# Early table entries and gathers placed later, the last logits placed before the early products, and a weight prefetch placed before later table entries

## The chip, the core and the metric

The kernel runs on one core of a Trainium2 chip. The metric is the device time of one execution in microseconds, the median of the runs shown. The core has five engines, each with its own queue of instructions that it works through in order: PE (matrix products), DVE (vector operations), ACT (activations and copies), POOL (here mostly DMAs with computed addresses) and SP, which issues the ordinary DMAs. All DMAs run on 16 DMA engines.

## What is computed

One layer of a diffusion backbone over 1024 latent tokens and 256 context tokens of width 1024: two token mixers (a state-space scan and windowed attention), an output projection with a gated residual, and then a mixture of 32 experts. Only the last two matter here:

```python
x = x + g1 * (concatenate([ssd_x, attn_x], axis=-1) @ w_out)
h2 = rms_norm(x, norm2) * (1 + sc2) + sh2
# each token: the best of 4 groups, then the best 2 of its 8 experts
g_prob = softmax(h @ w_group + b_group);  g_w, g_idx = top_k(g_prob, 1)
e_w, e_idx = top_k(softmax(e_logits[g_idx]), 2)
expert = g_idx * 8 + e_idx
# per expert, over its tokens, weighted and summed back into the tokens
y = (silu(xb @ w_gate[e]) * (xb @ w_up[e])) @ w_down[e]
return rms_norm(x + g2 * moe_x, norm_final)
```

All is float32; `w_gate`, `w_up` and `w_down` hold 32 experts with 6 MB each.

## The kernel before

The tokens stand in 8 blocks of 128. `out_all` (L966) is the output projection and the routing. For each block `b`, `out_a` prepares the operands of block `b + 1`; `out_b` (L900) makes the 48 products of the projection on PE, adds the residual on DVE (L912, L913), stores the rows into `acc` (L914), takes the root mean square on ACT (L918, L919), scales the rows on DVE (L920, L922), adds a shift (L923, on POOL, for the last block on DVE) and stores them into `h2d` (L924). `out_c` (L945), called one block behind, transposes the rows on PE (L949), copies them to SBUF (L951, L953), makes the router's logits (L956) and adds their bias on DVE (L957).

`route_to` routes the blocks in three groups that end before blocks 4, 6 and 8. `route` finds each token's two experts and its place among the expert's tokens, and POOL scatters one entry (token, weight) for each into a table in DRAM, `tab`, with one indirect DMA (L1093) for each block and choice: 8, 4 and 4 of them. `counts` counts the tokens of each expert; `place_ranks` sorts the experts by this count on DVE (L1118 to L1128) into a list `ovf`. For all places but the first two, the expert is known only from this list: SP reads it into a register (`expert_at`), both for a weight load and for a load of table entries.

The first two places are always experts 0 and 1 (`FIXED = 2`). They are worked on early, for the tokens of blocks 0 to 3 alone: `early_tables` loads their entries of `tab` with four DMAs on SP (L1237), `early_gather` computes row numbers on DVE (L1241) and gathers the rows of `h2d` on POOL (L1273), `early_x` transposes them, `early_gu` makes their gate and up products on PE (L1304, 64 instructions in the profile for each expert). Experts 0 and 1 get a second place for the tokens of blocks 4 to 7 (numbers 33 and 34), so the places are worked on in the order 0, 1, 33, 34, 2, 3, 4 and so on. A place has 64 slots ("half", two DMAs for its entries) or 128 (one DMA).

Weights come in chunks of 1 MB, six for each expert (two of gate, two of up, two of down), loaded on SP (L1256) into 7 buffers `wr` and 6 buffers `wl`. `prefetch(k)` issues loads in the order of use up to the k-th chunk, as long as by the program's own count a buffer is free. `wl` takes the space of the projection's weights and exists only after the last block. 7 chunks are asked for during the blocks and 12 right behind them, which are all chunks of experts 0 and 1. The chunks of full places are then split into two parts on ACT (L184) and DVE (L185); half places use them as they are.

`moe` (L1537) follows: it loads the entries of 33 and 34 (`tables_to(2 * FIXED)`), the gate `g2` and `g2h`, then `early_rest` finishes the early products (silu L1314, multiply L1315, transposes L1323, down products L1332, weighting L1337, add to `acc` by an indirect DMA L1341) and calls `place_ranks` between the multiply and the transposes. Then come the gathers of 33 and 34, table entries of further places, and the steps of the expert stage, of which each product step calls `prefetch` for all chunks again and gives buffers free.

The order of the instructions on a queue is drawn up when the program is built. A scheduler takes, for each engine, what is ready by its own estimate of the times, and of several the one that stands first in the code. So the order in the code is a priority and not the order itself. What touches the same tile or DRAM tensor waits for what stands before it in the code: a scatter into `tab` waits for an earlier load from it.

Of the kernel before, what the change touches and what calls it, by code (L numbers as in the profile page):

```python
# [21 lines left out]
NBX = NT // P  # L22
# [20 lines left out]
NX, TABLE_AHEAD = 3, 3  # L43
# [17 lines left out]
FIXED, MID, REST = 2, 13, 14  # L61
# [4 lines left out]
EARLY, NVX = 4, NE + FIXED  # L66
# [63 lines left out]
class Kern:  # L130
# [834 lines left out]
    def out_all(self):  # L965
        part, h2 = self.out_a(0), None  # L966
        self.out_mod()
        for b in range(NBX):
            nxt = self.out_a(b + 1) if b + 1 < NBX else None
            if b + 2 < NBX:  # L970
                self.out_load(b + 2)
            if b == EARLY + 2:
                self.early_gather()
            n2 = self.out_b(b, part)
            self.prefetch(min(NR, (3 * b + 4) // 2))
            if h2 is not None:
                self.out_c(b - 1, h2)
                self.route_to(b)
            if b == EARLY + 1:
                self.early_tables()  # L980
            part, h2 = nxt, n2
        self.oa.close()
        self.wop.close()
        self.wl = self.pool("wl", "right")
        self.prefetch(FIXED * NCH)
        self.early_x()
        self.early_gu(0, 0, 2)
        self.out_c(NBX - 1, h2)
        self.early_gu(0, 2, 4)
        self.early_gu(1, 0, 1)  # L990
        self.route_to(NBX)
        self.counts()
        self.early_gu(1, 1, 4)


    def first_max(self, dst_m, dst_i, src, m, n):
# [541 lines left out]
    def moe(self):  # L1538
        blocks = [b for _, bl in self.items for b in bl]
        at = lambda q: self.items[q][1]  # L1540
        X, A, T, Y, Z, G = {}, {}, {}, {}, {}, {}
        done = rows = tabs = FIXED
        nb = len(blocks)
        add = lambda b: self.half_add(Z.pop(b), b) if self.half(b) else self.y_add(Z.pop(b), self.lst[:, b, :])

        def x_ahead(q):

            for b in at(q):
                k = blocks.index(b)
                X[b] = self.half_x(k) if self.half(b) else self.x_t(k)  # L1550
                rows_to(k + NX + 1)
                gather_to(k + NX + 1)
                rows_to(k + NX + 2)
                tables_to(k + NX + 1 + TABLE_AHEAD)

        def gather_to(n):
            nonlocal done
            for i in range(done, min(n, nb)):
                self.gather(i, self.lst[:, blocks[i], :], blocks[i])
                done = i + 1  # L1560

        def rows_to(n):
            nonlocal rows
            for i in range(rows, min(n, nb)):
                self.half_rows(blocks[i])
                rows = i + 1

        def tables_to(n):
            nonlocal tabs
            for i in range(tabs, min(n, nb)):  # L1570
                self.lst_load(blocks[i])
                tabs = i + 1

        tables_to(2 * FIXED)
        self.g2 = self.mod_load(self.mp, 3, "g2")
        self.g2h = self.mp([512], "g2h")
        for n in range(2):
            self.nc.sync.dma_start(out=self.g2h[n * H:n * H + H], in_=self.modd[3][None, n * 512:n * 512 + 512].to_broadcast([H, 512]))
        self.early_rest()
        rows_to(2 * FIXED)  # L1580
        gather_to(2 * FIXED)
        tables_to(FIXED + NX + 1 + TABLE_AHEAD)
        x_ahead(FIXED)
        for t in self.steps:
            k, q = t[0], t[1] if len(t) > 1 else None
            p = self.items[q][0] if q is not None else None
            if k == "gu":
                if q == FIXED + 1 and t[2] == 0:
                    self.overflow()
                if t[2] == 0:  # L1590
                    for b in at(q):
                        G[b] = self.bank2(name="pgu")
                wg, wu = self.parts_for(p, (2 * t[2], 2 * t[2] + 1), (0, 0, 2, NW)[t[2]])
                for b in at(q):
                    if self.half(b):
                        self.half_gu(t[2], X[b], *((wg, wu) if self.half(p) else (wg[2], wu[2])), G[b])
                    else:
                        self.gu(t[2], X[b], wg, wu, G[b])
            elif k == "act":
                for b in at(q):  # L1600
                    A[b] = (self.half_act if self.half(b) else self.act)(G.pop(b))
            elif k == "x":
                x_ahead(q)
            elif k == "hT":
                for b in at(q):
                    T[b] = (self.half_h if self.half(b) else self.h_t)(A.pop(b))
                    Y[b] = self.bank2(name="py")
            elif k == "down":
                w, = self.parts_for(p, (8 + t[2],), 0)
                for b in at(q):  # L1610
                    if self.half(b):
                        self.half_down(T[b], w if self.half(p) else w[2], Y[b], t[2])
                    else:
                        self.down(T[b], w, Y[b], t[2])
            elif k == "y":
                for b in at(q):
                    Z[b] = self.half_y(Y.pop(b), b) if self.half(b) else self.y_out(Y.pop(b), self.lst[:, b, :])
                    if p != REST - 1:
                        add(b)
            elif k == "rest":  # L1620
                self.moe_rest()
                self.rested = True
                for b in list(Z):
                    add(b)
            elif k == "final":
                self.final()
            elif k == "last":
                self.final_rows(Y.pop(p))
# [249 lines left out]
```

## Time and profile before

| | |
|---|---|
| time, median of 3 runs | 1314.62 us (1313.06 to 1315.48) |
| the profiled execution, its own time | 1314.99 us |
| its span, first to last instruction | 1313.2 us |
| PE busy | 1175.0 us (89%) |
| DVE busy | 801.9 us (61%) |
| ACT busy | 577.9 us (44%) |
| POOL busy | 338.8 us (26%) |
| DMA, mean over the span | 255 GB/s, 335.08 MB |
| mean granted clock of TensorE | 0.957 of full speed |

How to read it: the profile is of one execution, times are from the span's start. "PE busy" counts a product from its start to a modelled end. In a timeline a row is one instruction or a run of like ones: start, duration, engine, line of the kernel, operation, "output<-inputs" by the program's names, count, and in brackets how long the engine had stood idle before it and what ended that. For SP the rows are DMA issues; the duration is that of the issue, not of the transfer. In a table of windows each row is a stretch of time with the busy time of each engine, the granted clock of TensorE (1.00 is 2.4 GHz, 0.50 is 1.2 GHz), the share of the DMA engines' time and the rate.

### The profile page before, as it was taken

How to read it: one execution, taken by the hardware profiler on the slowest of the kernel's cores; microseconds unless marked ns; L12 is line 12 of the kernel's file. 1: busy time of each engine (PE TensorE's matmuls, PEld its weight loads, DVE VectorE, ACT ScalarE, POOL GpSimd, SP SyncE). 2: the span in 40 equal slices, each digit the busy share in tenths (PEclk: the TensorE clock that was granted, in tenths of full speed). 3: DMA queues.
4: the chain of work that ended last, by engine and by line, in shares of the span. 5: the costliest groups of instructions: out<-in, count | busy, mean ns of one | idle time of the engine just before them, and what ended most of it. 6: DMA issues, size and time to landing. Idle time of an engine off the chain costs nothing. (4 is left out here: it accounts for less than half of the span.)

```text
span 1313.2 us, 19111 instructions
## 1 busy us (share of the span) xinstructions
PE 1175.0 (89%) x6806; PEld 845.4 (64%) x6806; DVE 801.9 (61%) x1392; ACT 577.9 (44%) x1046; POOL 338.8 (26%) x295
## 2 busy tenths in 40 slices
PE   5799999888798999899997989999999999989881
PEld 2678778878786666588764556555556665556550
DVE  1688885678957877565566525454546545566543
ACT  5643333355547766433340423343334443454423
POOL 0250000477723444211414111112112121121110
PEclk9699999999988999999999999998999999999996
DMA  9665644866333300494354999999869999999866
GB/s 336 246 211 190 212 137 127 260 226 208 124 117 100 97 25 16 148 339 167 121 212 123 404 405 402 369 360 383 324 225 417 405 401 404 375 401 367 333 216 271
DMA packets 105185, 335.08 MB, mean 255 GB/s; under 512 B 20152, under 2 KB 38584, under 8 KB 80512
## 3 DMA queue, kind: packets, MB, share of 16 engines
q1 hardware_dynamic: 95024, 314.82, 63.6%
q0 software_dynamic: 9328, 17.10, 5.4%
q10 hardware_dynamic: 736, 1.92, 0.4%
q8 instruction: 54, 0.88, 0.3%
q14 instruction: 43, 0.35, 0.1%
HBM read 299.75 MB, written 43.47 MB: 261 GB/s over the span
## 5 line engine op out<-in xcount | busy, mean ns | idle before, releaser
L185 DVE TENSOR_TENSOR wl<-wf,wh 128x1024 fp32r<-128x1024 f32 x180 | 213.2, 1221 | 79.5 <-ACT wh L184 74.0
L184 ACT CAST wh<-wf 128x1024 fp32r<-128x1024 f32 x180 | 180.9, 1052 | 119.5 <-PE pgu L1367 94.5
L1304 PE MATMUL pgu<-wf,xT 128*64 128x256 f32 x1280 | 166.5, 393 | 0.8 <-DVE yeh L1337 0.4
L1304 PEld LDWEIGHTS pgu<-wf,xT 128*64 128x64 f32 x1280 | 92.2, 140 | 60.8 <-issue 17.3
L471 PE MATMUL pzq<-xw,hxh 128*128 128x256 f32 x512 | 100.6, 296 | 0.0
L1367 PE MATMUL pgu<-wl,xh 128*128 128x512 f32 x240 | 83.5, 412 | 14.2 <-DVE wl L185 14.1
L1367 PE MATMUL pgu<-wh,xh 128*128 128x512 f32 x240 | 83.8, 423 | 8.8 <-ACT wh L184 8.8
L773 POOL TENSOR_SCALAR p<-p,sst 128x640 f32<-128x640 f32 (+1 forms) x32 | 66.1, 2067 | 98.9 <-DVE sst L770 53.5
L1341 POOL DMA_INDIRECT acc<-yeh,hrow x19 | 40.0, 2104 | 188.5 <-DVE yeh L1337 160.8
L1332 PE MATMUL py<-wf,hTh 128*64 128x512 f32 x320 | 80.5, 622 | 5.3 <-ACT hTh L1325 4.8
L471 PEld LDWEIGHTS pzq<-xw,hxh 128*128 128x128 f32 x512 | 83.5, 197 | 1.0 <-issue 0.2
L1367 PE MATMUL pgu<-wh,xl 128*128 128x512 f32 x240 | 77.3, 402 | 0.0
L352 PE MATMUL pxb<-hxh,xw 128*128 128x512 f32 x256 | 76.4, 397 | 0.0
L1403 POOL DMA_INDIRECT acc<-ye,lst x15 | 26.8, 1786 | 189.4 <-DVE ye L1399 104.9
L471 PE MATMUL pzq<-xw,hxl 128*128 128x256 f32 x256 | 74.4, 290 | 0.0
L1393 PE MATMUL py<-wh,hT 128*128 128x512 f32 x240 | 70.4, 401 | 2.0 <-ACT hT L1385 1.9
L1367 PEld LDWEIGHTS pgu<-wh,xh 128*128 128x128 f32 x240 | 43.1, 191 | 41.1 <-ACT wh L184 27.4
L756 DVE TENSOR_REDUCE sst<-psc 128x1 f32<-128x640 f32 (+1 forms) x64 | 50.4, 789 | 29.9 <-PE psc L755 24.9
L1367 PEld LDWEIGHTS pgu<-wl,xh 128*128 128x128 f32 x240 | 46.1, 192 | 34.6 <-DVE wl L185 23.9
L759 ACT ACTIVATE p<-psc,sst 128x640 f32<-128x640 f32 (+1 forms) x64 | 49.2, 770 | 15.1 <-DVE sst L770 7.7
L1337 DVE SCALAR_TENSOR_TENSOR yeh<-py,lst,g2h 128x512 f32<-128x512 f32 x20 | 15.0, 750 | 64.5 <-PE py L1332 63.3
L1367 PEld LDWEIGHTS pgu<-wh,xl 128*128 128x128 f32 x240 | 46.3, 193 | 11.7 <-issue 2.4
(366 smaller groups left out, 2524.5 us busy)
## 6 DMA issues: line engine op xcount, KB each, us to landing
wf<-in_w_gate SPq DMA_DIRECT2D x64, 1024.0 KB
wf<-in_w_up SPq DMA_DIRECT2D x64, 1024.0 KB
wf<-in_w_down SPq DMA_DIRECT2D x64, 1024.0 KB
wa<-in_w_ada SPq DMA_DIRECT2D x48, 512.0 KB
R<-csd SPq DMA_DIRECT2D x16, 512.0 KB
xl<-xd SPq DMA_DIRECT2D x17, 256.0 KB
xt<-in_x SPq DMA_DIRECT2D x8, 512.0 KB
xf<-in_w_xbc SPq DMA_DIRECT2D x8, 512.0 KB
```

Of the source, the lines that this page charges most:

```text
L184: self.nc.scalar.copy(hi, src)
L185: (eng or self.nc.vector).tensor_tensor(lo, src, hi.bitcast(F32), OP.subtract)
L352: nc.tensor.matmul(px[s], w(wp, kc), self.hx(hp, kc, s, 512), start=st, stop=sp)
L471: nc.tensor.matmul(ps, self.hx(hp, kc, b // 4, P, (b % 4) * P), w(wp, kc), start=kc == 0 and hp + wp == 0, stop=kc == KC - 1 and hp == 1)
L756: v.tensor_reduce(mx, ps[:, o:512 + nl], AX.X, OP.max)
L759: nc.scalar.activation(p_[:, :NCX + nl], ps[:, o:512 + nl], AF.Exp, bias=nm, scale=0.125, accum_out=den)
L773: (v if j % 2 else nc.gpsimd).tensor_scalar(p_, p_, den[:, j - i:j - i + 1], None, op0=OP.mult)
L1304: self.nc.tensor.matmul(pg[n * H:n * H + H, o:o + 256], xT[:, i0 + kk, a * H:a * H + H], w[:, kk * 512 + n * 256:kk * 512 + n * 256 + 256] ...
L1332: self.nc.tensor.matmul(py[n * H:n * H + H, 0:512], hT[:, i, a * H:a * H + H], w[:, n * 512:n * 512 + 512], start=f == 0, stop=f == 3)
L1341: self.nc.gpsimd.indirect_dma_start(out=self.acc.rearrange("t (a c) -> (t a) c", a=2), out_offset=bass.IndirectOffsetOnAxis(ap=self.hrow[: ...
L1367: nc.tensor.matmul(pg[:, n * 512:(n + 1) * 512], x[xp][:, k, :], w[wp][:, kk * 512:(kk + 1) * 512], start=k == 0 and xp + wp == 0, stop=k ...
L1393: nc.tensor.matmul(py[:, n * 512:(n + 1) * 512], hT[:, hp, f, :], wd[wp][:, n * 512:(n + 1) * 512], start=f == 0 and hp + wp == 0, stop=f ...
```

## The change

Three things are moved; no operation is added or taken away.

1. In `out_all` the call of `early_tables` goes from the end of block 5 to block 6, right behind `out_b(6)`, and the call of `early_gather` from block 6 to block 7, both ahead of `out_b` of its block.
2. Behind the blocks, `out_c` of the last block goes ahead of `early_x` and of all early products. The products are then cut in two calls, expert 0 ahead of the last routing and expert 1 behind the counts.
3. In `moe`, behind the gathers of 33 and 34, `prefetch(len(self.order))` is called ahead of the next table entries, and these are asked for up to the 7th place of the list instead of the 9th; the remaining two follow in `x_ahead(FIXED)`, the next call.

```diff
--- before.py
+++ after.py
@@ -969,28 +969,26 @@
             nxt = self.out_a(b + 1) if b + 1 < NBX else None
             if b + 2 < NBX:
                 self.out_load(b + 2)
-            if b == EARLY + 2:
+            if b == NBX - 1:
                 self.early_gather()
             n2 = self.out_b(b, part)
+            if b == EARLY + 2:
+                self.early_tables()
             self.prefetch(min(NR, (3 * b + 4) // 2))
             if h2 is not None:
                 self.out_c(b - 1, h2)
                 self.route_to(b)
-            if b == EARLY + 1:
-                self.early_tables()
             part, h2 = nxt, n2
         self.oa.close()
         self.wop.close()
         self.wl = self.pool("wl", "right")
         self.prefetch(FIXED * NCH)
+        self.out_c(NBX - 1, h2)
         self.early_x()
-        self.early_gu(0, 0, 2)
-        self.out_c(NBX - 1, h2)
-        self.early_gu(0, 2, 4)
-        self.early_gu(1, 0, 1)
+        self.early_gu(0, 0, 4)
         self.route_to(NBX)
         self.counts()
-        self.early_gu(1, 1, 4)
+        self.early_gu(1, 0, 4)
 
 
     def first_max(self, dst_m, dst_i, src, m, n):
@@ -1579,7 +1577,8 @@
         self.early_rest()
         rows_to(2 * FIXED)
         gather_to(2 * FIXED)
-        tables_to(FIXED + NX + 1 + TABLE_AHEAD)
+        self.prefetch(len(self.order))
+        tables_to(2 * FIXED + 3)
         x_ahead(FIXED)
         for t in self.steps:
             k, q = t[0], t[1] if len(t) > 1 else None
```

## Rows read from the trace of the kernel before

**Rows 1.** Page, the span in 40 slices: busy tenths of the DMA engines

```profile
DMA  9665644866333300494354999999869999999866
```

**Rows 2.** Windows: us, busy us of PE, PEld, DVE, ACT, POOL; PEclk, DMA, GB/s

```profile
690.00:700.00 10.00, 9.02 (x58) 4.09 (x56) 4.30 (x12) 1.13 (x3) 6.11 (x6) 1.00 0.03 1
...
700.00:710.00 10.00, 7.63 (x42) 3.95 (x40) 8.31 (x33) 1.07 (x2) 4.03 (x4) 0.83 0.44 113
...
710.00:720.00 10.00, 8.10 (x68) 4.72 (x64) 7.29 (x24) 0.38 (x1) 4.70 (x4) 0.97 0.62 190
...
720.00:730.00 10.00, 6.76 (x34) 2.88 (x36) 5.00 (x5) 4.26 (x5) 0.00 (x0) 0.69 1.00 405
...
950.00:960.00 10.00, 10.00 (x56) 6.26 (x54) 4.66 (x6) 4.21 (x7) 0.00 (x0) 1.00 0.56 210
```

**Rows 3.** Timeline of SP's DMA issues: start us, us, what, count

```profile
647.30 2.47 SPq L1237 DMA_DIRECT2D lst<-tab  x4
...
663.87 0.32 SPq L924 DMA_DIRECT2D h2d<-ot  x1
...
664.29 0.38 SPq L1256 DMA_DIRECT2D wf<-in_w_up  x1
...
672.48 0.32 SPq L914 DMA_DIRECT2D acc<-xr  x1
...
696.67 2.39 SPq L1237 DMA_DIRECT2D lst<-tab  x4
...
706.27 7.79 SPq L1237 DMA_DIRECT2D lst<-tab  x8
...
714.24 0.45 SPq L1256 DMA_DIRECT2D wf<-in_w_gate  x1
...
715.18 0.09 SPq L1256 DMA_DIRECT2D wf<-in_w_up  x1
...
726.71 0.33 SPq L1256 DMA_DIRECT2D wf<-in_w_up  x1
```

**Rows 4.** Timeline of DVE; in brackets the idle time before and its releaser

```profile
649.97 0.22 DVE L1241 TENSOR_SCALAR hrow<-lst,C 128x1 int32<-128x1 int32 x1 [4.65 <-DMA lst<-tab]
...
677.27 0.16 DVE L920 RECIPROCAL xss<-xss 128x1 f32<-128x1 f32 x1 [3.79 <-ACT xss L919]
...
678.78 1.22 DVE L923 TENSOR_TENSOR ot<-ot,sh 128x1024 f32<-128x1024 f32 x1
...
682.94 0.26 DVE L957 SCALAR_TENSOR_TENSOR lg<-plg,xss,V 128x36 f32<-128x36 f32 x1 [2.33 <-PE plg L956]
...
694.11 1.21 DVE L1122 TENSOR_REDUCE rsm<-rsq 128x32 f32<-128x1024 f32 x1
...
699.23 0.21 DVE L1241 TENSOR_SCALAR hrow<-lst,C 128x1 int32<-128x1 int32 x1 [3.90 <-DMA lst<-tab]
...
704.41 0.75 DVE L1337 SCALAR_TENSOR_TENSOR yeh<-py,lst,g2h 128x512 f32<-128x512 f32 x1 [1.17 <-DMA g2h<-modd]
```

**Rows 5.** Timeline of PE

```profile
674.16 3.67 PE L1304 MATMUL pgu<-wf,xT 128*64 128x256 f32 x32 [0.19 <-ACT xT L1294]
...
677.76 1.09 PE L949 MATMUL ph2T<-C,xr 128*128 128x128 f32 x8
...
704.64 0.75 PE L1293 MATMUL pxe<-C,xa 128*128 128x128 f32 x4 [2.18 <-DMA xa<-h2d,hrow]
```

**Rows 6.** Timeline of POOL

```profile
665.28 1.03 POOL L1093 DMA_INDIRECT tab<-pay,rows  x1 [1.44 <-DVE rows L1089]
...
694.53 0.96 POOL L1093 DMA_INDIRECT tab<-pay,rows  x1 [0.30 <-issue]
```

**Rows 7.** Timeline of ACT

```profile
674.00 1.06 ACT L918 ACTIVATE junk<-xr 128x1024 bf16<-128x1024 f32 x1
...
693.36 0.38 ACT L1314 ACTIVATE sghg<-pgu 128x256 f32<-128x256 f32 x1 [4.92 <-PE pgu L1304]
...
721.87 1.04 ACT L184 CAST wh<-wf 128x1024 fp32r<-128x1024 f32 x1 [5.42 <-DMA wf<-in_w_up]
```

## The prediction

> **What bounds the kernel now.** I first read the page's slices: a slice is 1313.2 / 40 = 32.8 us, and from slice 22 (722 us) on the DMA engines stand at 9 tenths with few dips [rows 1]. That is the expert stage: by the code 32 x 6 weight chunks of 1 MB go through SP's queue. The 10 us stretches show its start [rows 2]: a DMA share of 0.03 in 690-700, 0.44 and 0.62 in the next two, then 1.00 at 405 GB/s. So the stream rests ahead of a stage that it bounds. In 950-960 the share is 0.56 and PE is busy for all 10 us; there the chunks' buffers come free too late. PE got there at the pace of the weights, so a stream that starts earlier should move that stretch as well.
>
> SP's instructions [rows 3] say why it rests. Twelve chunks fit the early work. SP then waits for the experts' ranks, issues eight table loads from 706.27 on (7.79 us), and only then the thirteenth chunk, at 714.24. DVE [rows 4] shows what the ranks wait for. The last block's logits (L957) come at 682.94; routing and scatters follow; the next table entries land at 699.23 after 3.90 us of waiting; the ranks' last parts stand behind that wait in DVE's queue and behind the multiply at 704.41, with the cast that SP reads right behind. PE [rows 5] shows why the logits are late: the early products' first 32 instructions (674.16, 3.67 us) stand ahead of the last block's transposes at 677.76. POOL and ACT [rows 6, 7] give the scatters, the end of the early products and the first weight split.
>
> **Part 1, last logits ahead of the early products.** The last block's rows are ready when SP stores them at 672.48 [rows 3]. ACT squares them at 674.00 only, behind the first early copy [rows 7]; this copy now comes later, so the square can start up to 1.5 us earlier. The transposes can run at about 673 instead of 677.76. On DVE [rows 4] the logits stand behind the reciprocal (677.27) and the add that ends at 678.78 + 1.22 = 680.00, then waited 2.33 us for PE. Without PE's lateness they come at 680.0 at the latest, with the earlier square at 678.5: 2.9 to 4.4 us earlier. Scatters (last one 694.53 [rows 6]) and the table loads at 696.67 [rows 3] follow at the same distance, so I take 4.
>
> Not all of it reaches SP. The second early product's silu (693.36, it waited 4.92 us for PE [rows 7]) feeds a DVE multiply that stands ahead of the reduction at 694.11 [rows 4]. PE has the same work in another order, so its end stays; I add 1 us for a later gather (part 3). The reduction then starts at 695.1 and ends at 696.3; the entries have landed, so what followed 699.23 starts at 696.3, 2.9 us earlier. The multiply's constants (1.17 us of waiting at 704.41) move by 4 and hold nothing. **I take 3.0 us** at SP's 706.27; the bounds are 0 (PE's early work ends 4 us late) and 4.4.
>
> **Part 2, chunks ahead of later entries.** The code says "all chunks", but there are 6 + 7 = 13 buffers and 12 are full: exactly one chunk passes the tables. Table issues after it stay eight (five now, three in the next step), so the fourteenth keeps its place, 0.94 us behind the old thirteenth [rows 3]. What is won is a chunk moved during the table loads, while the share is 0.44 to 0.62: 1.049 MB / 405 GB/s = **2.6 us** less in front of the stream. Bounds: 0 if the stream starves afterwards, 3.6 if the first chunk would have moved at the pace of 710-720, part of it shared with gathers. I take 2.6, the pace of the full stretch. Starving is the question: a few chunks followed the one at 715.18, and then none until 726.71 [rows 3], when PE had freed a buffer. PE was held by a copy of ACT behind the first split, which stood 5.42 us for the first chunk until 721.87 [rows 7]. That chunk now lies there long before, so the next issue comes earlier too.
>
> The first chunk needs the same register load as the first table; the loads behind it are eight DMA issues with the same wait. They are read by gathers and by small DVE row computations; if they are late, the overflow arithmetic on DVE is next to wait, and behind it the late half block's product.
>
> The Trainium skill's "DMA: Bandwidth & Descriptors" (section "Queues, rings and completion order") says that each DMA engine takes the descriptors of one ring in ring order. By that the first two or three tables land up to a chunk later; no row here has a lone table load behind a chunk on a free DVE.
>
> **Part 3, early entries and gathers later.** Removed: SP's wait and four loads at 647.30 (2.47 us) between the fifth and seventh block's stores, DVE's 4.65 us wait at 649.97 [rows 4]. Both engines had nothing due there: PE runs its products through. So the gain is between 0 and 0.2 us, and I take 0. Added: four loads, two row computations and two gathers at a later place. SP's order is by readiness, not by code alone: the eighth chunk (664.29) goes ahead of the store at 672.48 [rows 3], which the code has first. So the entries may well stay near 647. If they come behind the store at 663.87, the next scatters (665.28 [rows 6]) must wait for these reads, the gathers stand behind four scatters, and land near 677, after the 674.16 at which PE uses them now [rows 5]. PE would do the last block's transposes and logits meanwhile. Cost 0 to 3 us at the end of the early products, of which I took 1 in part 1.
>
> **Sum.** -3.0 - 2.6 = -5.6 us. The profiled execution took 1314.99 (span 1313.2), 0.4 over the median of 1314.62; off the median it gives 1309.0.
>
> **Rivals.** *Only the chunk counts.* PE's early products end 3 us later or more, because the gather is late and PE idles; after idling its granted clock drops, as in 720-730 (0.69, with 6.76 us busy [rows 2]). The ranks then gain nothing: -2.6 us, 1312. Against it: the last block's transposes and logits (1.09 us at 677.76, and the logits behind) fill that very hole.
>
> *Nothing moves, the change does not do what it says.* Queue order by readiness puts everything back, the chunk lands late among gathers, or the consumption-bound stretch at 950 gives the gain back: 1314.6, within 1.5. For it: one chunk is 0.5% of the stream. Against: the order of PE in [rows 5] follows the code.
>
> *Slower.* The early entries fall behind the eighth chunk's issue at 664.29. They land near 671 with that chunk ahead; DVE's row computation waits in front of the last block's eviction, the four scatters start at 671 instead of 665.28, the gathers land near 682, the early products start near 683 instead of 674.16. They need 693.4 - 674.2 = 19 us less some 3 for the last block's work, 16 us, and 2 more after the idle clock: the silu comes at 701 instead of 693.36, SP gets the ranks 5 to 6 us late, and the chunk gives 2.6 back: +3, 1317.6. It decides from a landing of about 680 on. Against it: the entries' data are there from 647.30, and SP, which goes by readiness, waits for a late store ahead of 663.87.
>
> *Late tables.* If the tables behind the chunk land 2.6 us later and DVE waits for them in front of the late half block's multiply, PE frees buffers that much later and the stream may starve for 2 to 3 us: 1311.5.
>
> The ring order of the page named above is a reason for this last one; whether DVE then has to wait no row here shows.
>
> **How the numbers follow.** Forecast (1306.5 to 1311.5) 0.55; only the chunk 0.12; late tables 0.08; nothing 0.13; slower 0.12. About 0.2% (2.6 us) is what a measurement of this kernel can tell from no change. Below 1312.0 lie the forecast, most of late tables and half of "only the chunk": 0.68. Within 0.2%: 0.20. Slower: 0.12. The range 1304.5 to 1316.5 takes in both upper bounds (4.4 + 3.6 = 8 us, and 2 more for a restarted clock) and all but the slower case.
>
> **What would show it.** Right: L957 of the last block near 679; the silu that was at 693.36 within 2 us of it; the SP chunk near 703 ahead of its table loads, and DMA busy there; the first split well before 721.87; the stretches from 730 on the same, some 6 us earlier, to the end. Part 1 is wrong if the cast is not earlier though the logits are; part 2 if the fourteenth chunk comes later than the ranks allow or DMA goes idle behind the first five; part 3 if the early transposes come after 678. The forecast as a whole is wrong if the shift at 730 is there and lost by 1250.

## The result, and the profile after

The changed kernel takes 1304.23 us (median of 7 runs, 1300.81 to 1311.00) against 1315.28 (7 runs, 1313.01 to 1317.07) for the kernel before beside it: a ratio of **0.993, 95% interval 0.9902 to 0.9957**. The ratio comes from all runs of a comparison and is not the quotient of the two medians: the kernel is faster by 9 us by the ratio and by 11 by the medians, where 5.6 were forecast. In a later comparison the ratio was 0.9902 (0.9873 to 0.9931), 13 us. One execution of e2 and one of e11 below were far longer, at a lower granted clock, and the ratios leave them out. The profiled execution, the fastest of the seven, took 1300.81 us, its span is 1299.0 and its mean granted clock 0.962.

Both profiles run in step until the store into `h2d` that answers to 663.87 in [rows 3] (663.99 after). What differs comes behind it, so times of the two can be compared as they stand. First the 10 us windows of the changed kernel, columns as in [rows 2]:

```profile
690.00:700.00 10.00, 8.97 (x52) 3.73 (x50) 4.00 (x10) 1.13 (x3) 4.87 (x5) 1.00 0.39 116
700.00:710.00 10.00, 8.01 (x50) 4.58 (x48) 8.45 (x32) 2.12 (x3) 4.42 (x3) 0.83 0.44 112
710.00:720.00 10.00, 10.00 (x84) 6.41 (x80) 8.35 (x21) 3.59 (x5) 3.15 (x3) 1.00 0.95 364
720.00:730.00 10.00, 10.00 (x62) 7.18 (x58) 2.76 (x5) 2.84 (x6) 2.66 (x2) 1.00 1.02 403
```

Two things are to be seen. The weight stream is at full share one window earlier than in [rows 2]. And PE is busy for 8.01 + 10 + 10 = 28.0 us of 700 to 730, where it was busy for 7.63 + 8.10 + 6.76 = 22.5 before, and the granted clock of 0.69 in 720-730 is gone.

SP's DMA issues after, against [rows 3] (lines are two lower in the changed file):

```profile
647.43 2.46 SPq L1235 DMA_DIRECT2D lst<-tab  x4
...
692.26 2.39 SPq L1235 DMA_DIRECT2D lst<-tab  x4
...
697.72 0.37 SPq L1254 DMA_DIRECT2D wf<-in_w_gate  x1
698.27 8.27 SPq L1235 DMA_DIRECT2D lst<-tab  x8
...
709.62 0.34 SPq L1254 DMA_DIRECT2D wf<-in_w_up  x1
...
717.11 0.33 SPq L1254 DMA_DIRECT2D wf<-in_w_up  x1
```

The early entries have not moved (647.43 against 647.30). The ranks reach SP at 697.72 instead of 706.27, 8.55 us earlier. One chunk passes the tables, as forecast; the next comes only at 709.62, 11.9 us behind it and 5.6 earlier than its counterpart at 715.18. The chunk that went out at 726.71 [rows 3] goes out at 717.11, 9.6 us earlier.

DVE after, against [rows 4], shows where 8.55 us come from:

```profile
677.21 0.25 DVE L957 SCALAR_TENSOR_TENSOR lg<-plg,xss,V 128x36 f32<-128x36 f32 x1
677.38 1.22 DVE L923 TENSOR_TENSOR ot<-ot,sh 128x1024 f32<-128x1024 f32 x1
...
687.76 1.22 DVE L1120 TENSOR_REDUCE rsm<-rsq 128x32 f32<-128x1024 f32 x1
...
692.58 0.42 DVE L1313 TENSOR_TENSOR sghg<-sghg,pgu 128x256 f32<-128x256 f32 x1 [2.35 <-ACT sghg L1312]
...
694.82 0.21 DVE L1239 TENSOR_SCALAR hrow<-lst,C 128x1 int32<-128x1 int32 x1 [0.68 <-DMA lst<-tab]
...
696.29 0.16 DVE L1126 CAST ovf<-rsm 1x32 int32<-1x32 f32 x1
...
700.93 0.75 DVE L1335 SCALAR_TENSOR_TENSOR yeh<-py,lst,g2h 128x512 f32<-128x512 f32 x1 [3.87 <-DMA g2h<-modd]
```

The last logits come 5.7 us earlier and now stand ahead of the shift (L923). The ranks' first reduction (L1122 before, L1120 now) stands ahead of the second silu's multiply, and the cast that SP reads ahead of the weighted product (L1335), which waits 3.87 us for `g2h`.

PE after, against [rows 5]:

```profile
672.86 1.07 PE L949 MATMUL ph2T<-C,xr 128*128 128x128 f32 x8
...
677.41 7.13 PE L1302 MATMUL pgu<-wf,xT 128*64 128x256 f32 x64
...
704.00 0.72 PE L1291 MATMUL pxe<-C,xe 128*128 128x128 f32 x4 [1.99 <-DMA xe<-h2d,hrow]
```

ACT after, against [rows 7]: the second silu came at 692.16 (before 693.36), and the first weight split at 705.24 instead of 721.87.

```profile
692.16 0.38 ACT L1312 ACTIVATE sghg<-pgu 128x256 f32<-128x256 f32 x1 [7.20 <-PE pgu L1302]
...
705.24 1.05 ACT L184 CAST wh<-wf 128x1024 fp32r<-128x1024 f32 x1
```

So the fourteenth chunk is 5.6 us ahead, the number of the forecast, but four chunks later the lead is 9.6 us. And the lead is not fixed then: on PE it grows between two groups of transposes. Timeline of PE, the kernel before:

```profile
767.22 0.50 PE L1323 MATMUL phT<-C,hgh 128*128 128x128 f32 x2
...
773.49 1.23 PE L1354 MATMUL pxe<-C,xe 128*128 128x128 f32 x8
775.70 0.75 PE L1293 MATMUL pxe<-C,xa 128*128 128x128 f32 x4 [0.98 <-DVE xl L1357]
777.16 0.93 PE L1354 MATMUL pxe<-C,xe 128*128 128x128 f32 x4 [0.72 <-DMA xe<-h2d,lst]
778.03 4.64 PE L1304 MATMUL pgu<-wf,xT 128*64 128x256 f32 x28
...
806.69 0.75 PE L1383 MATMUL phT<-C,hg 128*128 128x128 f32 x4
```

and the same stretch of work after:

```profile
758.58 0.50 PE L1321 MATMUL phT<-C,hgh 128*128 128x128 f32 x2
...
764.86 0.63 PE L1352 MATMUL pxe<-C,xe 128*128 128x128 f32 x3
765.42 1.52 PE L1302 MATMUL pgu<-wf,xT 128*64 128x256 f32 x12
766.87 0.88 PE L1352 MATMUL pxe<-C,xe 128*128 128x128 f32 x5
767.67 1.95 PE L1302 MATMUL pgu<-wf,xT 128*64 128x256 f32 x16
769.55 0.75 PE L1291 MATMUL pxe<-C,xa 128*128 128x128 f32 x4
...
792.58 0.75 PE L1381 MATMUL phT<-C,hg 128*128 128x128 f32 x4
```

PE is 8.6 us ahead at the first group and 14.1 at the second. Its way from one to the other takes 806.69 - 767.22 = 39.5 us before and 792.58 - 758.58 = 34.0 after. Before, PE did the transposes of the next two places first and waited for them; after, 28 products of a half place go ahead of them and none of these rows waits. This was in no step of the prediction; the experiments ask what it is and what it is worth. The profile's end is 14.2 us earlier.

### The profile page after: what moved, and what is told of

The parts are those of the page before. It is cut to its first block, busy times and chain, and to the rows that moved or that the text cites. A ratio compares the mean times of both kernels' runs of the same rounds, so it can differ in the third digit from the quotient of the medians.

```text
span 1299.0 us, 19112 instructions
## 1 busy us (share of the span) xinstructions
PE 1168.1 (90%) x6806; PEld 845.9 (65%) x6806; DVE 802.5 (62%) x1392; ACT 575.5 (44%) x1044; POOL 339.1 (26%) x295
## 5 line engine op out<-in xcount | busy, mean ns | idle before, releaser
L1302 PE MATMUL pgu<-wf,xT 128*64 128x256 f32 x1280 | 162.2, 388 | 0.5 <-DVE yeh L1335 0.4
L1302 PEld LDWEIGHTS pgu<-wf,xT 128*64 128x64 f32 x1280 | 91.1, 138 | 57.2 <-issue 11.9
L1365 PE MATMUL pgu<-wl,xh 128*128 128x512 f32 x240 | 83.2, 410 | 14.2 <-DVE wl L185 14.1
L1339 POOL DMA_INDIRECT acc<-yeh,hrow x19 | 39.5, 2080 | 176.1 <-DVE yeh L1335 137.0
L1335 DVE SCALAR_TENSOR_TENSOR yeh<-py,lst,g2h 128x512 f32<-128x512 f32 x20 | 15.0, 749 | 68.7 <-PE py L1330 64.8
L1391 PEld LDWEIGHTS py<-wh,hT 128*128 128x128 f32 x240 | 43.7, 191 | 16.9 <-issue 5.1
```

The lines of the kernel that those rows point to most:

```text
L1302: self.nc.tensor.matmul(pg[n * H:n * H + H, o:o + 256], xT[:, i0 + kk, a * H:a * H + H], w[:, kk * 512 + n * 256:kk * 512 + n * 256 + 256] ...
L1339: self.nc.gpsimd.indirect_dma_start(out=self.acc.rearrange("t (a c) -> (t a) c", a=2), out_offset=bass.IndirectOffsetOnAxis(ap=self.hrow[: ...
L1365: nc.tensor.matmul(pg[:, n * 512:(n + 1) * 512], x[xp][:, k, :], w[wp][:, kk * 512:(kk + 1) * 512], start=k == 0 and xp + wp == 0, stop=k ...
L1391: nc.tensor.matmul(py[:, n * 512:(n + 1) * 512], hT[:, hp, f, :], wd[wp][:, n * 512:(n + 1) * 512], start=f == 0 and hp + wp == 0, stop=f ...
```

## The experiments

Executions differ in length already ahead of the change, and the kernel before had medians of 1314.6 to 1320.0 us from one comparison to the next. So across runs only two things are compared: ratios to the kernel before on the same chip, and times in a profile less the shift of the store that stands at 663.87 in [rows 3] (**shift** in the table behind the first seven runs).

**e1, the last logits alone.** Part 1 of the change without parts 2 and 3.

```diff
         self.prefetch(FIXED * NCH)
+        self.out_c(NBX - 1, h2)
         self.early_x()
-        self.early_gu(0, 0, 2)
-        self.out_c(NBX - 1, h2)
-        self.early_gu(0, 2, 4)
-        self.early_gu(1, 0, 1)
+        self.early_gu(0, 0, 4)
         self.route_to(NBX)
         self.counts()
-        self.early_gu(1, 1, 4)
+        self.early_gu(1, 0, 4)
```

> Part 1 alone (last logits ahead, products cut anew), chunk still behind eight table loads. Theory A (the ranks' time sets the start, buffers set the rest): SP gets the ranks near 697.7 as in the changed kernel, the thirteenth chunk goes out near 706, the fourteenth near 709.6 when PE frees its buffer, so the stream is as early as in the changed kernel and the time is 9 to 11 us under the kernel before, within 2 us of the changed kernel. Rival B (the two parts add): 2.6 us slower than the changed kernel, 6 to 8 us under the kernel before. Theory C (a part of the gain comes later, from PE's order of transposes near 770, which this kernel shares): the lead over the kernel before grows from about 7 us at 730 to over 12 at 985.

Measured: 1304.90 us, ratio 0.9913 (0.9887 to 0.994). This part alone has the whole gain, as far as the intervals tell. Rival B (6 to 8 us) lies at the edge of the interval (7.9 to 14.9 us), and the lead grows as theory C has it: less the shift, PE is 8.0 us ahead at the first group of transposes and 13.4 at the second.

**e2, the chunk alone.** Part 2 without parts 1 and 3.

```diff
-        tables_to(FIXED + NX + 1 + TABLE_AHEAD)
+        self.prefetch(len(self.order))
+        tables_to(2 * FIXED + 3)
         x_ahead(FIXED)
```

> Part 2 alone (thirteenth chunk ahead of the table loads), ranks at 706.3 as before. Theory A: thirteenth chunk near 706.3, fourteenth still near 715, stream 2.6 to 3.6 us earlier, time 2 to 4 us under the kernel before. Rival B: 2.6 us. Theory C: PE's order near 770 is that of the kernel before, so the lead stays at 2 to 4 us to the end. If the chunk only delays the gathers of places 33 and 34: no change.

Measured: 1312.91 us, ratio 0.9944 (0.9926 to 0.9963). SP's issues in this run:

```profile
703.67 0.37 SPq L1256 DMA_DIRECT2D wf<-in_w_gate  x1
704.22 8.49 SPq L1237 DMA_DIRECT2D lst<-tab  x8
712.97 0.37 SPq L1256 DMA_DIRECT2D wf<-in_w_up  x1
...
720.47 0.33 SPq L1256 DMA_DIRECT2D wf<-in_w_up  x1
```

Its store stands at 661.01, so 2.86 us of every difference are not the change's. The chunk goes out 7.7 us earlier than the thirteenth of before (714.24 - 703.67 - 2.86); the fourteenth not at all (715.18 - 712.97 = 2.2, less 2.86). The chunk of 726.71 goes out at 720.47, 3.4 us earlier less the shift, but six chunks later nothing is left of that (732.09 here, 734.55 before). So the stream as a whole gains little. What is won is on PE, in the window that had 6.76 us busy and a clock of 0.69 before:

```profile
720.00:730.00 10.00, 10.00 (x70) 6.65 (x66) 5.87 (x7) 4.40 (x6) 2.67 (x2) 1.00 1.00 404
```

The ratio is a gain of 7.4 us (4.9 to 9.8), more than any of the theories had.

**e3, parts 1 and 2 without part 3.** The hunks around `early_tables` and `early_gather` are left out.

> The changed kernel with the early table entries and gathers back at their old places in the code. If readiness alone orders them, nothing changes: within 0.3% of the changed kernel, table loads near 647.4 in both. If the place mattered: up to 1 us.

Measured: 1308.78 us, ratio 0.9918 (0.9895 to 0.9941). All five queues have the order of the changed kernel, so this is also a second measurement of it: the parts' ratios (0.9913 and 0.9944) do not add.

**e4, the cast held back.** The changed kernel, with the ranks' cast put behind the first weighted product on DVE, as it stood before the change.

```diff
-        v.tensor_copy(self.ovf[:, 3, :], pe[0:1])
+        self.pe = pe
...
             self.half_add(self.half_y(py, b), b)
+            if b == 0:
+                i = self.nc.vector.tensor_copy(self.ovf[:, 3, :], self.pe[0:1])
+                self.tc.add_manual_dep(i.ins, self.yi.ins.name, mybir.DependencyInfo(mybir.DependencyClass.NoSync, mybir.DependencyReason.DATA), reason="ranks behind the first product")
```

> The changed kernel, but the cast that hands the ranks to SP is held behind the first early product's weighting on DVE, where the kernel before has it; PE's order of transposes near 770 becomes that of the kernel before too. Theory A: SP's chunk near 702.8 instead of 697.7, fourteenth near 711.5 instead of 709.6, stream 2 us later than in the changed kernel at 730. Theory C: the lead does not grow after that, so 5 to 7 us under the kernel before in all. Without C: 7 to 9 us under it.

Measured: 1307.04 us, ratio 0.9913 (0.9895 to 0.9932). SP gets the ranks at 704.66, with a shift of 2.5: 4.1 us earlier than before instead of 8.6. The ratio is that of e1 and e3. The cast now waits behind the weighted product, and that for `g2h`:

```profile
702.80 0.75 DVE L1335 SCALAR_TENSOR_TENSOR yeh<-py,lst,g2h 128x512 f32<-128x512 f32 x1 [3.63 <-DMA g2h<-modd]
703.47 0.16 DVE L1536 CAST ovf<-rsm 1x32 int32<-1x32 f32 x1
```

Half of the gain at SP, which I had taken for the path, can be taken away without a loss that these runs can tell.

The fourteenth chunk is also a poor measure of the stream: e4's is 4.3 us behind that of e1, the 18th 2.6 and the 31st 0.2. One expectation failed: PE's order near 770 did not go back to that of before, so e4 says nothing of what that order is worth, and its gain of 11.5 us is above what either theory had.

All of e1, e3, e4 and the changed kernel have the 28 products ahead of the transposes near 770; e2 and the kernel before have them behind. The next run moves this alone.

**e5, the order near 775 alone.** The kernel before; the first transposes of place 8 of the list are made to follow the last product of place 6. The instruction lists of DVE, ACT, POOL and SP are those of before, and on PE one group changes its place.

```diff
-            nc.tensor.transpose(ps[:, i, :], xv[:, i, :], self.ident)
+            t = nc.tensor.transpose(ps[:, i, :], xv[:, i, :], self.ident)
+            if k == 8:
+                self.tc.add_manual_dep(t.ins, self.gi.ins.name, mybir.DependencyInfo(mybir.DependencyClass.NoSync, mybir.DependencyReason.DATA), reason="behind the products of place 6")
...
-                    self.nc.tensor.matmul(pg[n * H:n * H + H, o:o + 256], xT[:, i0 + kk, a * H:a * H + H],
+                    self.gi = self.nc.tensor.matmul(pg[n * H:n * H + H, o:o + 256], xT[:, i0 + kk, a * H:a * H + H],
```

> The kernel before with one thing moved on PE alone: near 775 us the last 28 products of the second early-list half place (place 6 of the list) go ahead of the transposes of place 8, as in every variant that has the last logits first; all other queues keep their order. Theory C (the later gain is this order, a by-product of the new schedule): the transposes no longer wait 0.98 and 0.72 us and the products do not run at half clock; PE's way from its transposes at 767.22 to those at 806.69, 39.5 us before, takes about 34, and the end comes 4 to 6 us earlier: ratio 0.9955 to 0.997. Theory E (the later gain comes from the stream's earlier start and has nothing to do with this order): the same 39 us or the wait goes elsewhere, ratio 0.999 to 1.001.

Measured: 1312.23 us, ratio **0.9939 (0.9921 to 0.9957)**, against a median of 1319.99 for the kernel before. PE in this run:

```profile
765.71 0.50 PE L1325 MATMUL phT<-C,hgh 128*128 128x128 f32 x2
...
771.98 1.23 PE L1356 MATMUL pxe<-C,xe 128*128 128x128 f32 x8
773.14 3.24 PE L1306 MATMUL pgu<-wf,xT 128*64 128x256 f32 x28
776.31 0.75 PE L1293 MATMUL pxe<-C,xa 128*128 128x128 f32 x4
776.90 0.65 PE L1356 MATMUL pxe<-C,xe 128*128 128x128 f32 x4
...
799.35 0.75 PE L1385 MATMUL phT<-C,hg 128*128 128x128 f32 x4
```

No transposes wait, the 28 products take 3.24 us instead of 4.64, and the way takes 33.6 us. Theory C holds, and the order is worth somewhat more than the 4 to 6 us expected, though the interval takes in 6: 0.61% is 8 us (5.7 to 10.4), and the two profiles' ways differ by 39.47 - 33.64 = 5.8. The rest is open. Nothing of the change's text is in this kernel.

**e6, the chunk and this order.** e2 with the edit of e5.

> The chunk ahead of the tables alone, with the same move on PE. The chunk alone had 0.9944. Theory C: the two add, about 4 us more, ratio near 0.991, as with the logits alone; the way between the two groups of transposes falls from 38.6 to about 34 us. Theory E: ratio stays at 0.994 to 0.995.

Measured: 1305.92 us, ratio 0.9905 (0.9874 to 0.9935). The two add, within their intervals (0.56% and 0.61% alone, 0.95% together), and the last logits are not needed to come down to the changed kernel's time.

**e7, part 3 alone.**

```diff
-            if b == EARLY + 2:
+            if b == NBX - 1:
                 self.early_gather()
             n2 = self.out_b(b, part)
+            if b == EARLY + 2:
+                self.early_tables()
...
-            if b == EARLY + 1:
-                self.early_tables()
```

> Part 3 alone, the early entries and gathers a block or two later in the code. All theories: the queues keep the order of before, so ratio 0.999 to 1.001 and the entries are loaded near 647 us. Theory C: PE waits again near 775 us for the transposes, as in the profile before, and takes 38 to 40 us between the two groups of transposes. If that profile was a chance of one execution, it takes about 34.

Measured: 1320.32 us, ratio 1.0004 (0.9985 to 1.0023). This is a second profile of before's queues, and PE waits at the same place, with the products as fast as in e5 this time:

```profile
781.09 0.75 PE L1293 MATMUL pxe<-C,xa 128*128 128x128 f32 x4 [0.96 <-DVE xl L1357]
782.53 0.72 PE L1354 MATMUL pxe<-C,xe 128*128 128x128 f32 x4 [0.69 <-DMA xe<-h2d,lst]
783.18 3.24 PE L1304 MATMUL pgu<-wf,xT 128*64 128x256 f32 x28
```

**The runs side by side.** "14th" is the issue of the fourteenth chunk and "PE" the first group of transposes above, both against before (715.18 and 767.22) and less the shift; "way" is from that group to the second, and "2nd" the second group (806.69 before) less the shift.

| kernel | shift | 14th | PE | way | 2nd | ratio |
|---|---|---|---|---|---|---|
| before | 0 | 0 | 0 | 39.5 | 0 | 1 |
| e7, part 3 | 4.0 | +0.2 | +1.4 | 37.9 | -0.2 | 1.0004 |
| e5, order | -1.2 | +0.1 | -0.3 | 33.6 | -6.2 | 0.9939 |
| e2, chunk | -2.9 | +0.7 | -3.8 | 38.6 | -4.7 | 0.9944 |
| e6, chunk and order | 0 | +0.5 | -5.8 | 35.0 | -10.3 | 0.9905 |
| e1, logits | 1.8 | -8.2 | -8.0 | 34.0 | -13.4 | 0.9913 |
| e4, cast held back | 2.5 | -3.9 | -7.8 | 33.7 | -13.6 | 0.9913 |
| after | 0.1 | -5.7 | -8.8 | 34.0 | -14.2 | 0.993 |
| e3, as after | 6.6 | -5.6 | -7.4 | 34.0 | -12.9 | 0.9918 |

The ways fall into two classes: 33.6 to 35.0 us with the products ahead, 37.9 to 39.5 with the transposes ahead, whatever else is moved (the last four runs, with the products ahead, took 35.3 to 35.6). What the order itself takes away is idle time of PE: 5.2 to 5.9 us of the way with the transposes ahead (before, e7, e2), 3.0 with the products ahead, in all of these runs. The chunk and the order add at the second group as well: 4.7 and 6.2 us alone, 10.3 together. And within the intervals the ratio goes with PE and its way, not with the fourteenth chunk: e2 and e6 gain with a chunk that is no earlier, e4 loses nothing with one 4 us later than e1's.

**e8 to e11, is the chunk ahead of the tables worth anything here, and is there a better version?** With the logits first the chunk seemed to pay nothing, and PE waited 1.99 us for the gather of place 34. e8 and e10 are the changed kernel with `g2` loaded later, so that `g2h` is issued first; e9 is the changed kernel beside e10; e11 is e1 with the same move, that is without the chunk ahead.

```diff
         tables_to(2 * FIXED)
-        self.g2 = self.mod_load(self.mp, 3, "g2")
         self.g2h = self.mp([512], "g2h")
...
         x_ahead(FIXED)
+        self.g2 = self.mod_load(self.mp, 3, "g2")
```

> The changed kernel with the gate g2 loaded behind the gathers of 33 and 34 and the next tables' calls, so that g2h is issued first and the first weighted product (it waited 3.87 us for g2h) comes some 0.7 us earlier. The weighted product is on nobody's way to the first products of 33: ratio as after, 0.990 to 0.994. If the add behind it or the freed bank is on the way, up to 1 us better than that.

> The changed kernel once more, beside the two below on one chip. Its ratio was 0.993 (0.9902 to 0.9957), the same queues without part 3 had 0.9918: expected 0.992, within 0.9895 to 0.9945. PE's way between the two groups of transposes is again 34 to 35 us.

> The changed kernel with g2 loaded later, once more. If the later g2 is worth something, its ratio lies at least 0.0015 below that of the changed kernel beside it (0.9905 against 0.992); if it is worth nothing, the two agree within 0.001.

> The logits first and g2 later, without the chunk ahead of the tables. Theory A (with the logits first the chunk ahead pays nothing, since it only makes the gather of place 34 land 2 to 3 us late): PE does not wait for that gather (3.04 us in the kernel with the chunk ahead), the first products of 33 start about 2.5 us earlier than there, and so does the fourteenth chunk; ratio equal to the one beside it or up to 0.002 below. Rival (the chunk ahead pays as much here as alone, 0.9944): ratio 0.003 to 0.005 above it.

Measured: e8 0.9905 (0.9886 to 0.9924); in a later comparison e9 0.9902 (0.9873 to 0.9931), e10 0.9892 (0.9865 to 0.9918), e11 0.9882 (0.9849 to 0.9915). All four ratios lie where they were expected. Of the details, e9's way took 35.6 us instead of 34 to 35, and e11's fourteenth chunk came 1.5 us earlier than e10's, less the shifts, instead of 2.5. The later `g2` brings the weighted product's wait down (1.54 us in e8 instead of 3.87) and at the end 0.001 (e10 beside e9), less than the intervals. The runs speak against the rival, that the chunk pays as much on top of the logits as alone: e11 lies 0.001 below e10, not 0.003 to 0.005 above, and e1 no higher than e3. With intervals of some 0.003 to either side this is likely and not certain. The gather shows one thing that it costs. PE's transposes of the two gathered tiles in e8, with the chunk ahead:

```profile
697.52 0.75 PE L1291 MATMUL pxe<-C,xa 128*128 128x128 f32 x4 [0.37 <-DMA xa<-h2d,hrow]
701.30 1.10 PE L1291 MATMUL pxe<-C,xe 128*128 128x128 f32 x4 [3.04 <-DMA xe<-h2d,hrow]
```

and in e11, without it:

```profile
701.41 0.75 PE L1291 MATMUL pxe<-C,xa 128*128 128x128 f32 x4
702.00 0.65 PE L1291 MATMUL pxe<-C,xe 128*128 128x128 f32 x4
```

POOL issued that gather at 693.00 in e8 and at 697.31 in e11: 8.3 us until PE could use it with the chunk beside it, 4.7 at most without. In the other profiles with the chunk beside it (after, e3, e9, e10) it was 6.1 to 7.2 us; in e1 4.7 at most, and 4.6 in e4, where the chunk goes out 5.0 us behind the gather. No version is told apart from the changed kernel.

## Why the prediction was right in direction and too small

The direction and the place of the change's first effect were right. The fourteenth chunk is 5.6 us earlier where 5.6 was the sum, but that agreement is luck: one term was too small, the other paid nothing on top of it, and four chunks later the lead is 9.6 us. The gain is 1.6 to 2.3 times the forecast (9 and 13 us), in part because part 1 was sized too small and in part for a reason outside the sum.

**Part 1 ("I take 3.0 us at SP's 706.27").** The mechanism was right and the term was mis-sized: 8.55 us. The logits came 5.7 us earlier, not 4, because they went ahead of the shift at L923, behind which I had left them. And two instructions that I had assumed to stay in line behind late work did not: the reduction behind the second multiply, and the cast behind the first weighted product. In e4 the cast alone, put back, left 4.1 us of it; the product ahead of it waited 3.63 us for `g2h`, so the constants that in the prediction "hold nothing" held the cast there. I had read DVE's order off [rows 4] as if it were fixed, although it is drawn up anew for every program.

That SP's time is the path was the second error of this step. Between e1 and e4 the fourteenth chunk differs by 4.3 us and the ratio not at all. What the end seems to follow is whether PE has work between 700 and 730; this is argued from the table, and no run changed that alone.

**Part 2 ("a chunk moved during the table loads ... 2.6 us", "the fourteenth keeps its place, 0.94 us behind the old thirteenth").** Exactly one chunk passed, as said. The fourteenth did not keep its place: with the logits first it waited for a buffer that PE gave back (709.62, 11.9 us behind the thirteenth, after 2.8 us of waiting for PE's products of place 33), the starving named as the question. Alone (e2) it kept its place, and the gain came in another way than by a shorter stream: the first split no longer waits until 721.87 [rows 7], and PE does not idle at 720-730. Alone that is worth 3.8 us at 767, 4.7 at 807 and 0.56% (7.4 us) at the end; the rest of it is open. On top of part 1, which cures the same idle time, it is worth nothing that e1, e3 and e11 can tell. By this reading the two terms of the sum were added although both paid for the same hole on PE.

**Part 3 (0).** Right, by the reason given: the order on the queues did not change at all, the entries are loaded near 647 us, and e7 has a ratio of 1.0004. So the rival *slower*, which needed them behind the eighth chunk, had no place to start.

**The step that was missing.** The forecast said that the shift at 730 would stay "the same, some 6 us earlier, to the end". At 807 it is 14.1. A by-product of part 1 is another order on PE some 80 us later: products of a half place ahead of the next places' transposes. It is worth 0.61% by itself (e5), at least as much as the whole forecast of 5.6 us (0.43%). The changed kernel with the order of before put back was not run; that the order makes the later part of its gain rests on e5, e6 and the ways. The rows of before show its price to a reader who asks PE's timeline for waits behind 730: 0.98 and 0.72 us of idle time on work that was not due yet, and 28 products of 4.64 us instead of 3.24. These rows were there before the forecast was made, and I did not price them: in the windows a PE busy for 8.30 and 7.53 us of ten passed for the stream's pace. Why the scheduler's own estimate puts the products first when the logits come earlier was not tried; the order in the built lists shows that it does so with part 1 and not with parts 2 or 3.

**The other rivals.** *Only the chunk counts* needed a late end of the early products; the silu came 1.2 us earlier. *Nothing moves* is out. *Late tables*: the row computation behind the tables (709.41 after) did not wait, and up to 760 DVE waits for no table load. The ring order that the Trainium skill's "DMA: Bandwidth & Descriptors" (section "Queues, rings and completion order") states decided nothing for the tables. Another rule of that section, that each DMA engine takes turns between the queues which have work for it, bears on the gather: POOL's gather and SP's chunk would then share each engine, and the 6.1 to 8.3 us against 4.7 agree with it, though no run here separates this from other causes.

## What to carry to other kernels

Where a scheduler draws up the queues, a change in the order of the code is read from the new lists, engine by engine and to the end of the program, not only at the place of the edit; a gain or loss far behind the edit may be an order that came along by chance, and a single dependency that moves that order alone tells so. Two cures for the same idle stretch do not add: before summing, name the engine that idles and give the stretch to one of them. A PE wait on a transpose for a later place, with ready products queued behind it, is worth looking for by itself: here its removal was worth 0.61%, more than all that was planned.

## What was not expected of the hardware

After the same waits the clock did not fall at the same place. In the profile of before the products behind 0.98 and 0.72 us of idle time took 4.64 us, and the granted clock was below full from 770 to 800. In e7, with 0.96 and 0.69 us of idle time in the same places, they took 3.24, and the granted clock fell behind them, to 0.83 in 790 to 800. The products ahead do not spare PE that fall: each of the thirteen profiles has a window of 10 us between 770 and 820 with a granted clock of 0.83 to 0.89. In the changed kernel it is 810 to 820, behind the way. The ways as windows, columns as in [rows 2], first the kernel before and e7, with the transposes ahead:

```profile
767.22:806.69 39.47, 34.22 (x171) 21.22 (x169) 14.29 (x17) 12.01 (x17) 7.07 (x5) 0.91 1.01 401
```

```profile
772.61:810.47 37.86, 32.67 (x171) 20.88 (x169) 14.29 (x17) 12.01 (x17) 7.07 (x5) 0.95 1.02 403
```

and e5 and e9, with the products ahead:

```profile
765.71:799.35 33.64, 30.63 (x170) 19.54 (x169) 14.29 (x17) 12.12 (x17) 7.03 (x5) 1.00 1.02 407
```

```profile
760.88:796.46 35.58, 32.55 (x171) 20.84 (x169) 14.20 (x17) 12.11 (x17) 7.24 (x5) 0.95 1.02 405
```

PE stands idle for 5.25 and 5.19 us with the transposes ahead and for 3.01 and 3.03 with the products ahead, so 2.2 us of the way are the order's own in both pairs. The other 3.6 of the 5.8 us between before and e5 are PE's longer busy time at a clock of 0.91 instead of 1.00; between e7 and e9, both at 0.95, 0.1 us of that is left. So a way is no fixed price. But e7 is no further than before at the second group (0.2 us less the shift), although its way is 1.6 us shorter: its granted clock was 0.95 in 730 to 760 already, where before had 1.00, and it came to the first group 1.4 us later. In these two the losses to the clock lie at different places and come out alike, and they are better compared over the whole stretch than at one wait. Why e5 keeps its 6.2 us over both is shown for the 2.2 us of idle time; that the rest would come again in other executions is not.
